# Inverting the triangular blocks of a gated DeltaNet with powers of one nilpotent factor in place of three doublings

## The chip, the cores and the metric

The kernel runs on one core of a Trainium2 chip. Its time is the device time of one execution in microseconds, and lower is better. A core has five engines, each with a queue of its own that runs in order: PE multiplies matrices, DVE, ACT and POOL work on vectors, and SP issues the transfers. A profile records one execution.

## What is computed

Two layers, each a mixer of three parts that run side by side on the same projection (S5, gated DeltaNet or GDN, Mamba-2), an output projection, and a feed-forward part: dense in layer 0, eight experts in layer 1. There are 256 latent tokens behind 256 context tokens, 1024 wide. The change lies in GDN. For each chunk it solves a triangular system:

```
lower = jnp.where(strict, jnp.einsum("bhnid,bhnjd->bhnij", kb, k) * decay, 0.0)
rhs = jnp.concatenate([v * beta[..., None], kb * jnp.exp(gc)[..., None]], axis=-1)
sol = lax.linalg.triangular_solve(jnp.eye(CHUNK, dtype=F32) + lower, rhs,
                                  left_side=True, lower=True, unit_diagonal=True)
```

The kernel uses chunks of 128 tokens, four of them (t = 0 to 3), in two directions (d = 0, 1), with four heads in one tile of 128 x 512. It inverts the 128 x 128 matrix I + L of each head, and then walks over the chunks with a state for each direction.

## The kernel before

A mixer (`mixer`) projects the inputs (lines 336 and 784: product, convolution, SiLU), prepares GDN (`gdn_prep`, which inverts the blocks of 16 on the diagonal), and then writes down, one after another, GDN, the decays of Mamba-2, the remaining projections, the modulation vectors, S5's readout, Mamba-2's outputs and the output projection. That is not the order in which they run. Each part has a number (`band`), and a scheduler builds from these numbers, from the buffers and from modelled times one fixed order for every engine. Names that occur below:

- `inverses` (line 919) inverts two pairs (t, d) at once, a group. GDN has four groups, `grs[0]` to `grs[3]`, and after them or between them `step`, which uses an inverse, and `outs`, which normalizes the outputs `gd_o` by `gd_rs` and writes them (`gd_y`) to `yD`. From the blocks of 16 (`iv_X`) three levels lead to 128: at each, X is transposed and scaled to `iv_Z` (ACT), multiplied with `gd_kw` and masked to `iv_Q` (DVE), multiplied with X and subtracted from it (DVE).
- `m2_decays` (line 1060) computes 16 tiles of decays `dq_W`, writes them to `WD` in DRAM, and takes two selects `dq_r` on POOL for each (line 776). Mamba-2's outputs read them as `m_W`.
- `ada` (line 181) loads 32 pieces of 512 KB of layer 0's modulation weights, with two buffers, and accumulates them on PE in one bank of PSUM.
- `s5_out` (line 629) reads S5's states (`s5U`, `s5X`, `s5V`) and writes its part of `yD` as `s5yy`.
- The output projection reads `yD` as `yr`, splits it to `yo`, and multiplies it with `wH` and `wL`.
- Beside the projections DVE does the convolution's multiply-adds (`cv_acc`, line 800), the split of loaded weights (`wL`, line 322) and S5's scan (`s5B`, lines 609 and 612).

Each part has its tiles in a pool, and a pool is placed in SBUF at a fixed address of each partition. The decays' pool is on one side and GDN's on the other:

```
with self.band(b0 + q_["gd"]):
    p, q = self.pool("gd", sb)
    self.gdn(l, p, kT, qT, vD, kD, prep, *sc, qss, sm, szD, yD, t0, b0)
    q.close()
    qt.close()
with self.band(b0 + q_["db"]):
    p, q = self.pool("dq", sa)
    self.m2_decays(p, sm, WD, first)
```

In layer 0 the pool `dq` lies at 84992 to 101376 and `gd` at 102464 to 146400 (bytes of a partition in the compiled program). In layer 1 they are apart as well.

Of the kernel before, what the change touches and what calls it, by code (L numbers as in the profile page):

```python
# [10 lines left out]
F32 = mybir.dt.float32  # L11
F32R = mybir.dt.float32r
I32 = mybir.dt.int32
AF = mybir.ActivationFunctionType
OP = mybir.AluOpType
# [12 lines left out]
U0, QKV0, ZG0, ZM0, XBC0 = 0, 512, 2048, 2576, 3600  # L28

CST = ["ident", "ones", "le", "ge", "gt", "lt", "blk16"]  # L30
LEVELS = [16, 32, 64]

Q0 = dict(
    pb=1.0, sc=2.5, tl=1.5, th=0.5, nb=7.5, db=1.9, ab1=0.85, ab2=3.0, sb=3.5, u=1.02, st=0.6, qkv=1.0, g0=2.0,
# [19 lines left out]
def _cst():  # L54
    i = np.arange(128)
    r, c = i[:, None], i[None, :]
    out = [r == c, np.ones((128, 128)), r <= c, r >= c, r > c, r < c, r // 16 == c // 16]
    for b in LEVELS:
        mf = ((r // b) % 2 == 1) & (c // b == r // b - 1)
        out += [mf, mf.T]  # L60
    c16 = np.arange(16)[None, :]
    out += [c16 == r % 16, c16 > r % 16, c16 < r % 16, (r // 16) % 2 == np.arange(2)[None, :]]
    return np.concatenate([np.asarray(m, np.float32) for m in out], axis=1)
# [27 lines left out]
class Net:  # L91
    def __init__(self, ctx, tc, A, out, dump=None):
        self.tc, self.nc, self.A, self.out, self.dump = tc, tc.nc, A, out, dump or {}
        nc = self.nc
        self.cpool = ctx.enter_context(tc.tile_pool(name="const", bufs=1))
        self.wstack = ctx.enter_context(ExitStack())
        self.wpool = self.wstack.enter_context(tc.tile_pool(name="wts", bufs=2, side="right"))
        self.dram = ctx.enter_context(tc.tile_pool(name="scr", bufs=1, space=DRAM))
        self.psum = ctx.enter_context(tc.tile_pool(name="psum", bufs=1, space=PSUM))
        self.psum_split(mm=(0, 1), px=(2, 3), bg=(4, 5, 6, 7), ad=(6, 7))  # L100
        c = self.cpool
        ncst = len(CST) + 2 * len(LEVELS)
        cst = c.tile([128, ncst * 128 + NC16], F32, name="cst")
        self.bands, self.ma, self.cur = {}, {}, None
        nm = len(CST) * 128
        nc.sync.dma_start(cst[:, 0:nm], A["cst"][:, 0:nm])
        with self.band(1.7):
            nc.sync.dma_start(cst[:, nm:], A["cst"][:, nm:])

        def mat(j):  # L110
            return cst[:, j * 128:(j + 1) * 128]

        for j, n in enumerate(CST):
            setattr(self, n, mat(j))
        self.mt = {}
        for j, b in enumerate(LEVELS):
            self.mt[b, 0] = mat(len(CST) + 2 * j)
            self.mt[b, 1] = mat(len(CST) + 2 * j + 1)
        c16 = cst[:, ncst * 128:]
        self.id16, self.up16, self.lo16, self.half16 = c16[:, 0:16], c16[:, 16:32], c16[:, 32:48], c16[:, 48:50]  # L120
        self.tri_r = c.tile([128, 2, 128], F32R, name="tri_r")
        nc.vector.tensor_copy(self.tri_r[:, 0, :], self.gt)
        nc.vector.tensor_copy(self.tri_r[:, 1, :], self.lt)
        self.pp = [c.tile([128, NPP], F32, name=f"pp{l}") for l in range(2)]
        for l in range(2):
            with self.band(0 if l == 0 else 1.7):
                nc.sync.dma_start(self.pp[l], A["pp"][l])
        self.epst = c.tile([128, 1], F32, name="epst")
        nc.vector.memset(self.epst, EPS)
        self.mods = [c.tile([128, 48, 2], F32, name=f"mods{l}") for l in range(2)]  # L130
        self.xT = c.tile([128, KT, T], F32, name="xT")
# [461 lines left out]
    def s5_scan(self, l, p, B, lam):  # L593
# [25 lines left out]
        for q in range(4):  # L619
            gs = slice(q * 8, q * 8 + 8)  # L620
            for x in range(2):
                X = p.tile([128, 8, 64], F32, name="s5X", tag="s5t", bufs=Q[l]["st_"])
                nc.scalar.activation(X[0:64], bv[0:64, x, gs], AF.Copy)
# [271 lines left out]
    def gdn(self, l, p, kT, qT, vD, kD, prep, nrm, bs, ks, qss, sm, szD, yD, t0, b0):  # L895


        nc = self.nc
        kw, qw, x16 = prep
        first = t0 // 128  # L900
        sh = [128, 4, 128]

        def v4(ps):
            return ps.rearrange("p (h c) -> p h c", h=4)

        def col(m):
            return m.unsqueeze(2).to_broadcast(sh)

        def mm4(lhs, rhs):
            ps = self.ps()  # L910
            for h in range(4):
                self.mm(ps[:, h * 128:(h + 1) * 128], lhs(h), rhs(h), start=True, stop=True, skip_group_check=True)
            return ps
# [4 lines left out]

        def inverses(gr):

            X = {}
            for t, d in gr:
                X[t, d] = p.tile(sh, F32, name="iv_X", bufs=Q[l]["iv"])
                nc.gpsimd.tensor_tensor(X[t, d].rearrange("p h (b c) -> p h b c", c=16),
                                        x16[d][:, 4 * t:4 * t + 4].unsqueeze(2).to_broadcast([128, 4, 8, 16]),
                                        self.blk16.rearrange("p (b c) -> p b c", c=16).unsqueeze(1).to_broadcast([128, 4, 8, 16]),
                                        op=OP.mult)
            for b in LEVELS:
                Z, W = {}, {}
                for t, d in gr:  # L930
                    pz = self.ps()
                    for h in range(4):
                        nc.tensor.transpose(pz[:, h * 128:(h + 1) * 128], X[t, d][:, h], self.ident)  # L933
                    Z[t, d] = p.tile(sh, F32, name="iv_Z", tag="iv_Z", bufs=2)
                    for h in range(4):
                        nc.scalar.activation(Z[t, d][:, h], pz[:, h * 128:(h + 1) * 128], AF.Copy, scale=bs[:, t, d, h:h + 1])
                for t, d in gr:
                    pq = mm4(lambda h: kw[t][:, h], lambda h: Z[t, d][:, h])
                    W[t, d] = p.tile(sh, F32, name="iv_Q", tag="iv_Q", bufs=2)
                    nc.vector.tensor_tensor(W[t, d], v4(pq), self.mt[b, d].unsqueeze(1).to_broadcast(sh), op=OP.mult)  # L940
                for t, d in gr:
                    px = mm4(lambda h: W[t, d][:, h], lambda h: X[t, d][:, h])
                    nc.vector.tensor_tensor(X[t, d], X[t, d], v4(px), op=OP.subtract)
            return X

        def load(t):
# [6 lines left out]
        def step(t, d, Y, last):  # L953
# [5 lines left out]
            if old is not None:  # L959
                pr = mm4(lambda h: kT[:, h, sl], lambda h: old[:, h])  # L960
                r = p.tile(sh, F32, name="gd_r", bufs=1)
# [3 lines left out]
            else:  # L965
                r = vp[t]
# [4 lines left out]
                    nc.scalar.activation(qs[:, h], pqs[:, h * 128:(h + 1) * 128], AF.Copy, scale=cs[:, h:h + 1])  # L971
            pw = mm4(lambda h: Y[:, h], lambda h: r[:, h])
            if not last:
                vk = p.tile(sh, F32, name="gd_vk", tag="iv_Q", bufs=2)
                nc.vector.tensor_tensor(vk, v4(pw), col(ks[:, t, d, :]), op=OP.mult)
                pu = mm4(lambda h: ktk[t][:, h], lambda h: vk[:, h])
                if old is not None:
                    nc.gpsimd.tensor_tensor(old, old, col(sm["tot"][:, d, t, 16:20]), op=OP.mult)
                    nc.vector.tensor_tensor(old, v4(pu), old, op=OP.add)
                else:  # L980
                    S[d] = p.tile(sh, F32, name=f"gd_S{d}", bufs=1)
                    nc.scalar.activation(S[d], v4(pu), AF.Copy)
# [24 lines left out]
        def outs(pair):  # L1007

            f = slice(pair[0], pair[1] + 1)
            for t in pair:  # L1010
                for h in range(4):
                    jk = p.tile([128, 128], F32, name="gd_jk", bufs=1)
                    nc.scalar.activation(jk, os[t][:, h], AF.Square, accum_out=oss[:, t, h:h + 1])
            nc.vector.tensor_scalar(ov[:, f], qss[:, f], EPS, 128.0 * 128.0 * EPS, op0=OP.add, op1=OP.mult)
            nc.vector.tensor_add(ov[:, f], ov[:, f], oss[:, f])
            self.rsqrt(p, rs[:, f], ov[:, f], [128, 2, 4], 1.0 / 128, 0.0)
            for t in pair:
                nc.gpsimd.tensor_tensor(os[t], os[t], rs[:, t, :].unsqueeze(2).to_broadcast(sh), op=OP.mult)
            c = slice(pair[0] * 128 - t0, (pair[1] + 1) * 128 - t0)
            for h in (0, 2):  # L1020
                po = self.ps()
                for i in range(2):
                    for j, t in enumerate(pair):
                        nc.tensor.transpose(po[:, (2 * i + j) * 128:(2 * i + j + 1) * 128], os[t][:, h + i], self.ident)
                y = p.tile([128, 2, 256], F32, name="gd_y", tag="iv_Z", bufs=2)
                nc.sync.dma_start(y, szD[:, h:h + 2, c])
                nc.vector.scalar_tensor_tensor(y, po.rearrange("p (h c) -> p h c", h=2), self.prm(l, "gng"), y, op0=OP.mult,
                                               op1=OP.mult)
                nc.sync.dma_start(yD[:, 4 + h:6 + h, c], y)
# [966 lines left out]
```

## Time and profile before

| | |
|---|---|
| median of three runs | 2483.29 us (2481.88 to 2485.01) |
| profiled execution | 2479.87 us, span 2478.1 us |
| mean granted clock of PE | 0.974 of full speed |
| busy, of the span | PE 93%, DVE 75%, ACT 57%, POOL 10% |
| layer 0's mixer | 0 to about 716 us, then the dense part |
| layer 1's mixer | about 1200 to 1640 us, then the experts |
| transfers | 543.86 MB, mean 219 GB/s |

An engine's busy share is a mean over stages that have different limits, so the rows below are taken stage by stage. A time such as 397.15 is counted from the span's start. A group of rows names a line of the kernel, the tile that is written, and behind the arrow the tiles that are read; a `bank` is a piece of PSUM.

### The profile page before, as it was taken

The page shows a single profiled execution, that of the slowest core. Times are in us where ns is not written, and L with a number is a line of the kernel's source. Part 1 is how long each engine was busy: PE and PEld are TensorE (multiplying, and loading weights), DVE is VectorE, ACT ScalarE, POOL GpSimd, SP SyncE. Part 2 cuts the span into 40 slices and gives each one's busy share as a digit, 9 for nine tenths or more (in the row PEclk, how much of TensorE's full clock was granted, in tenths as well). Part 3 has the DMA queues.
Part 4 walks back from the last instruction along what each step waited for, and adds up shares of the span by engine and source line. Part 5 has one row for each costly group of instructions (what it writes and reads, how often), then busy time and mean ns, then how long its engine had stood idle before and what let it go on. Part 6 is the DMA issues. An engine that isn't in the chain of part 4 may idle for free.

```text
span 2478.1 us, 36217 instructions
## 1 busy us (share of the span) xinstructions
PE 2296.1 (93%) x12886; PEld 1843.6 (74%) x12886; DVE 1868.1 (75%) x3138; ACT 1419.7 (57%) x2200; POOL 257.3 (10%) x332
## 2 busy tenths in 40 slices
PE   7999887898999999998998799889999999999998
PEld 4878675666767777886887677778887888888876
DVE  8887995576577773436679867678888888888887
ACT  4765475343335343235764844357777777677765
POOL 0011553212000000000021522100000000000000
PEclk9999998997999999998999899989999999999999
DMA  7443336994455755323444474478999999999994
GB/s 254 134 125 121 112 122 215 268 277 146 122 204 176 255 179 185 94 89 101 149 135 130 157 209 123 133 290 316 332 335 362 349 338 337 356 342 341 354 344 167
DMA packets 222378, 543.86 MB, mean 219 GB/s; under 512 B 25584, under 2 KB 105456, under 8 KB 186096
## 3 DMA queue, kind: packets, MB, share of 16 engines
q1 hardware_dynamic: 222192, 541.49, 63.7%
q8 instruction: 103, 1.69, 0.3%
q14 instruction: 83, 0.68, 0.1%
HBM read 487.87 MB, written 53.54 MB: 218 GB/s over the span
## 4 chain that ended last, share of the span: by engine, by line
PE 65%; DVE 6%; DMA 5%; ACT 4%; issue 3%; POOL 0%; SPq 0%; ACTq 0%; DVEq 0%; POOLq 0%
PE bank L162 62%; DMA ada<-in_ada_w_dram 1%; ACT mwH L1673 1%; DVE mwL L1674 1%; DVE wL L322 1%; PE bank L1761 1%; DMA wr<-in_w_in_dram 1%; DVE s5B L612 0%; DMA s5X<-XD 0%; DVE s5t L609 0%; DVE cv_acc L800 0%; DMA vD<-gd_tok 0%; PE bank L933 0%; DMA s5V<-VD 0%; DMA yr<-yD 0%
## 5 line engine op out<-in xcount | busy, mean ns | idle before, releaser
L1674 DVE TENSOR_TENSOR mwL<-mwr,mwH 128x2048 fp32r<-128x2048 f32 (+1 forms) x272 | 605.1, 2226 | 96.5 <-PE bank L162 60.3
L1673 ACT ACTIVATE mwH<-mwr 128x2048 fp32r<-128x2048 f32 (+1 forms) x272 | 508.2, 1869 | 201.6 <-PE bank L162 168.8
L321 ACT ACTIVATE wH<-wr 128x512 fp32r<-128x512 f32 (+2 forms) x388 | 232.8, 605 | 389.6 <-PE bank L162 241.2
L322 DVE TENSOR_TENSOR wL<-wr,wH 128x512 fp32r<-128x512 f32 (+2 forms) x388 | 267.0, 690 | 209.5 <-ACT wH L321 204.7
L162 PE MATMUL bank<-mwL,xeH 128*128 128x512 f32 (+1 forms) x768 | 292.7, 381 | 9.3 <-DVE mwL L1674 9.3
L162 PE MATMUL bank<-mwH,xeL 128*128 128x512 f32 (+1 forms) x768 | 288.1, 375 | 0.0
L162 PE MATMUL bank<-mwH,xeH 128*128 128x512 f32 (+1 forms) x768 | 284.7, 376 | 2.5 <-ACT mwH L1673 2.5
L162 PE MATMUL bank<-hH,wH 128*128 128x512 f32 (+2 forms) x656 | 245.8, 383 | 32.0 <-ACT cv_acc L798 18.6
L162 PE MATMUL bank<-hH,wL 128*128 128x512 f32 (+2 forms) x656 | 245.6, 376 | 8.7 <-DVE wL L322 8.5
L162 PE MATMUL bank<-hL,wH 128*128 128x512 f32 (+2 forms) x656 | 246.6, 376 | 1.1 <-DVE hL L300 1.1
L162 PEld LDWEIGHTS bank<-mwL,xeH 128*128 128x128 f32 x768 | 144.3, 188 | 37.7 <-DVE mwL L1674 11.7
L162 PEld LDWEIGHTS bank<-hH,wH 128*128 128x128 f32 (+1 forms) x656 | 124.0, 190 | 61.7 <-ACT cv_acc L798 20.7
L162 PEld LDWEIGHTS bank<-mwH,xeH 128*128 128x128 f32 x768 | 144.1, 188 | 32.3 <-ACT mwH L1673 3.3
L162 PEld LDWEIGHTS bank<-mwH,xeL 128*128 128x128 f32 x768 | 144.3, 188 | 26.3
L800 DVE SCALAR_TENSOR_TENSOR cv_acc<-cv_raw,pp,cv_acc 128x512 f32<-128x512 f32 (+1 forms) x192 | 152.8, 811 | 7.5 <-ACT cv_acc L796 5.8
L162 PEld LDWEIGHTS bank<-hH,wL 128*128 128x128 f32 (+1 forms) x656 | 124.4, 190 | 33.7 <-DVE wL L322 10.7
L162 PE MATMUL bank<-yo,wH 128*128 128x512 f32 (+1 forms) x512 | 133.2, 351 | 11.5 <-ACT yo L1387 7.7
L162 PEld LDWEIGHTS bank<-hL,wH 128*128 128x128 f32 (+1 forms) x656 | 124.7, 190 | 25.3 <-DVE hL L300 2.9
L162 PE MATMUL bank<-fhH,wH 128*128 128x512 f32 x352 | 137.6, 394 | 2.7 <-ACT fhH L299 1.8
L162 PE MATMUL bank<-mwL,eaH 128*128 128x512 f32 x352 | 139.2, 395 | 0.0
L162 PE MATMUL bank<-mwH,eaL 128*128 128x512 f32 x352 | 138.6, 394 | 0.0
L162 PE MATMUL bank<-fhL,wH 128*128 128x512 f32 x352 | 137.9, 392 | 0.0
(449 smaller groups left out, 4531.2 us busy)
## 6 DMA issues: line engine op xcount, KB each, us to landing
mwr<-in_moe_gu_dram SPq DMA_DIRECT2D x176, 1024.0 KB, 5.7
mwr<-in_moe_dn_dram SPq DMA_DIRECT2D x80, 1024.0 KB, 6.0
wr<-in_w_in_dram SPq DMA_DIRECT2D x160, 256.0 KB, 2.9
ada<-in_ada_w_dram SPq DMA_DIRECT2D x24, 1024.0 KB, 7.1
wr<-in_w_out_dram SPq DMA_DIRECT2D x64, 256.0 KB, 2.7
ada<-in_ada_w_dram SPq DMA_DIRECT2D x32, 512.0 KB, 6.0
wr<-in_ffn_w_gate_dram SPq DMA_DIRECT2D x44, 256.0 KB, 2.7
wr<-in_ffn_w_up_dram SPq DMA_DIRECT2D x44, 256.0 KB, 2.8
```

The costliest lines, as they stand in the source:

```text
L162: return self.nc.tensor.matmul(*a, **k)
L321: nc.scalar.activation(wH, w, AF.Copy)
L322: nc.vector.tensor_tensor(wL, w, wH.bitcast(F32), op=OP.subtract)
L800: nc.vector.scalar_tensor_tensor(acc, raw[:, :, j:j + 256], w[:, j:j + 1], acc, op0=OP.mult, op1=OP.add)
L1673: nc.scalar.activation(wH, w, AF.Copy)
L1674: nc.vector.tensor_tensor(wL, w, wH.bitcast(F32), op=OP.subtract)
L1761: nc.tensor.transpose(pt[:, j * 128:(j + 1) * 128], a[:, j * 128:(j + 1) * 128], self.ident)
```

## The change

The three levels become one. X, the inverse of the diagonal blocks, is transposed and scaled once. Two products of it with `gd_kw`, each masked by one of two new masks (all blocks of 16 above, or below, the diagonal), give a nilpotent matrix G (tag `iv_Q`) and its transpose F (tag `iv_Z`). G2 = G·G comes from one more product. Then X becomes X − GX, X + G2·X, and X + G2·(G2·X). The tags `iv_Z` and `iv_Q` have three buffers instead of two, and the constants hold two masks in place of six (128 x 306 instead of 128 x 818 floats).

```diff
-LEVELS = [16, 32, 64]
...
-    for b in LEVELS:
-        mf = ((r // b) % 2 == 1) & (c // b == r // b - 1)
-        out += [mf, mf.T]
+    out += [c // 16 > r // 16, c // 16 < r // 16]
...
-            for b in LEVELS:
-                Z, W = {}, {}
-                for t, d in gr:
-                    pz = self.ps()
-                    for h in range(4):
-                        nc.tensor.transpose(pz[:, h * 128:(h + 1) * 128], X[t, d][:, h], self.ident)
-                    Z[t, d] = p.tile(sh, F32, name="iv_Z", tag="iv_Z", bufs=2)
-                    for h in range(4):
-                        nc.scalar.activation(Z[t, d][:, h], pz[:, h * 128:(h + 1) * 128], AF.Copy, scale=bs[:, t, d, h:h + 1])
-                for t, d in gr:
-                    pq = mm4(lambda h: kw[t][:, h], lambda h: Z[t, d][:, h])
-                    W[t, d] = p.tile(sh, F32, name="iv_Q", tag="iv_Q", bufs=2)
-                    nc.vector.tensor_tensor(W[t, d], v4(pq), self.mt[b, d].unsqueeze(1).to_broadcast(sh), op=OP.mult)
-                for t, d in gr:
-                    px = mm4(lambda h: W[t, d][:, h], lambda h: X[t, d][:, h])
-                    nc.vector.tensor_tensor(X[t, d], X[t, d], v4(px), op=OP.subtract)
+            for t, d in gr:
+                pz = self.ps()
+                for h in range(4):
+                    nc.tensor.transpose(pz[:, h * 128:(h + 1) * 128], X[t, d][:, h], self.ident)
+                Z[t, d] = p.tile(sh, F32, name="iv_Z", tag="iv_Z", bufs=3)
+                for h in range(4):
+                    nc.scalar.activation(Z[t, d][:, h], pz[:, h * 128:(h + 1) * 128], AF.Copy, scale=bs[:, t, d, h:h + 1])
+            for t, d in gr:
+                pg = mm4(lambda h: kw[t][:, h], lambda h: Z[t, d][:, h])
+                G[t, d] = p.tile(sh, F32, name="iv_Q", tag="iv_Q", bufs=3)
+                nc.vector.tensor_tensor(G[t, d], v4(pg), self.off[1 - d].unsqueeze(1).to_broadcast(sh), op=OP.mult)
+                pf = mm4(lambda h: Z[t, d][:, h], lambda h: kw[t][:, h])
+                F[t, d] = p.tile(sh, F32, name="iv_F", tag="iv_Z", bufs=3)
+                nc.vector.tensor_tensor(F[t, d], v4(pf), self.off[d].unsqueeze(1).to_broadcast(sh), op=OP.mult)
+            for t, d in gr:
+                p2 = mm4(lambda h: F[t, d][:, h], lambda h: G[t, d][:, h])
+                G2[t, d] = p.tile(sh, F32, name="iv_G2", tag="iv_Q", bufs=3)
+                nc.scalar.activation(G2[t, d], v4(p2), AF.Copy)
+                px = mm4(lambda h: G[t, d][:, h], lambda h: X[t, d][:, h])
+                nc.vector.tensor_tensor(X[t, d], X[t, d], v4(px), op=OP.subtract)
+            for t, d in gr:
+                px = mm4(lambda h: G2[t, d][:, h], lambda h: X[t, d][:, h])
+                nc.vector.tensor_tensor(X[t, d], X[t, d], v4(px), op=OP.add)
+            for t, d in gr:
+                px = mm4(lambda h: G2[t, d][:, h], lambda h: X[t, d][:, h])
+                tt = p.tile(sh, F32, name="iv_T", tag="iv_Z", bufs=3)
+                nc.scalar.activation(tt, v4(px), AF.Copy)
+                Z[t, d] = tt
+            for t, d in gr:
+                px = mm4(lambda h: G2[t, d][:, h], lambda h: Z[t, d][:, h])
+                nc.vector.tensor_tensor(X[t, d], X[t, d], v4(px), op=OP.add)
```

The tags' other users, `gd_vk` and `gd_y`, get `bufs=3` too. No band and no other part is edited. In layer 0 the pool `dq` now lies at 82944 to 99328 and `gd` at 98368 to 146400. The second buffer of `dq_r` (95232 to 99328) thus shares 960 bytes with GDN's `gd_ncs`, `gd_oss`, `gd_ov`, `gd_rs` and the start of its first `iv_X`. In layer 1 they don't meet. The scheduler makes the order anew. Lines of the new kernel are six lower than before up to `inverses` (776 is 770), and ten higher behind it (1018 is 1028).

POOL before, in layer 0: the last 16 selects (`dq_r`) stand among the projections' `cv_raw` and ahead of the third group's blocks (`iv_X`); the other 16 stand further ahead.

```order
L791 MEMSET cv_raw 128x2x2
L776 AFFINE_SELECT dq_r<-la_793 128x1024 x2
L790 MEMSET cv_raw 128x2x2
L791 MEMSET cv_raw 128x2x2
L776 AFFINE_SELECT dq_r<-la_793 128x1024 x14
L924 TENSOR_TENSOR iv_X<-gd_x_2935,cst 128x512
L924 TENSOR_TENSOR iv_X<-gd_x_2930,cst 128x512
L988 AFFINE_SELECT gd_A<-gd_qw_2866 128x512 x2
L1127 TENSOR_TENSOR m_S_5965<-m_S_5957,ex 128x512
```

POOL with the change, in layer 0: `gd_A` and `gd_o` are GDN's last steps and outputs.

```order
L998 AFFINE_SELECT gd_A<-gd_qw_2924 128x512
L988 TENSOR_TENSOR gd_S_3538<-gd_S_3538,ex 128x512
L998 AFFINE_SELECT gd_A<-gd_qw_2924 128x512
L998 AFFINE_SELECT gd_A<-gd_qw_2895 128x512
L1011 TENSOR_TENSOR gd_o<-gd_o,gd_qs 128x512 x2
L1028 TENSOR_TENSOR gd_o<-gd_o,gd_rs 128x512 x2
L770 AFFINE_SELECT dq_r<-la_793 128x1024 x19
L1197 TENSOR_TENSOR m_z<-m_in,m_z 128x4x128
L770 AFFINE_SELECT dq_r<-la_793 128x1024 x7
L1197 TENSOR_TENSOR m_z<-m_in,m_z 128x4x128
L770 AFFINE_SELECT dq_r<-la_793 128x1024 x6
L1158 TENSOR_TENSOR m_yo<-m_yo 128x512 x2
```

All 32 selects now stand behind the last `gd_o` (line 1028, which reads `gd_rs`), with two of Mamba-2's `m_z` among them.

PE before, where GDN's third group begins in layer 0 (line 933 transposes X, `iv_Z,gd_kw` is the first product of a level, `iv_X,iv_Q` the second).

```order
L933 MATMUL bank_3607<-cst,iv_X 128x128 x4
L933 MATMUL bank_3617<-cst,iv_X 128x128 x4
L162 MATMUL bank_3627<-iv_Z,gd_kw_2884 128x128 x3
L162 MATMUL bank_5365<-ada,sc 32x256 x4
L162 MATMUL bank_3627<-iv_Z,gd_kw_2884 128x128
L162 MATMUL bank_3634<-iv_Z,gd_kw_2913 128x128 x4
L162 MATMUL bank_3641<-iv_X,iv_Q 128x128 x4
L162 MATMUL bank_5365<-ada,sc 32x256 x4
L162 MATMUL bank_5599<-s5D,s5U 64x128
L162 MATMUL bank_3647<-iv_X,iv_Q 128x128 x4
L933 MATMUL bank_3653<-cst,iv_X 128x128 x4
```

PE with the change, at the same place.

```order
L926 MATMUL bank_3555<-cst,iv_X 128x128 x4
L926 MATMUL bank_3565<-cst,iv_X 128x128 x4
L156 MATMUL bank_3575<-iv_Z,gd_kw_2884 128x128 x4
L156 MATMUL bank_3582<-gd_kw_2884,iv_Z 128x128 x4
L156 MATMUL bank_3596<-gd_kw_2913,iv_Z 128x128
L156 MATMUL bank_3603<-iv_Q,iv_F 128x128 x4
L156 MATMUL bank_3596<-gd_kw_2913,iv_Z 128x128 x2
L156 MATMUL bank_3589<-iv_Z,gd_kw_2913 128x128 x4
L156 MATMUL bank_3596<-gd_kw_2913,iv_Z 128x128
L156 MATMUL bank_3610<-iv_X,iv_Q 128x128 x4
L156 MATMUL bank_3616<-iv_Q,iv_F 128x128 x4
L156 MATMUL bank_3623<-iv_X,iv_Q 128x128 x4
```

The modulation (`ada`) and S5 (`s5D`, `s5V`) stood between the products before; now the group stands by itself, and those rows come behind GDN and the decays.

SP before, in layer 0: the last decay writes to `WD`, the modulation loads, and S5's `XD`.

```order
L190 DMA ada<-in_ada_w_dram 128x4x256 x2
L1067 DMA WD_3090<-dq_W 128x512 x2
L320 DMA wr<-in_w_out_dram 128x512
L1067 DMA WD_3090<-dq_W 128x512 x3
L1335 DMA mD_94<-cvo 128x512
L1067 DMA WD_3090<-dq_W 128x512
L190 DMA ada<-in_ada_w_dram 128x4x256 x2
L1067 DMA WD_3090<-dq_W 128x512
L190 DMA ada<-in_ada_w_dram 128x4x256
L626 DMA XD_1897<-s5X 128x512
L190 DMA ada<-in_ada_w_dram 128x4x256
```

SP with the change, at the last decay writes.

```order
L1077 DMA WD_3090<-dq_W 128x512 x2
L1105 DMA m_in<-mD_94 128x4x128
L1077 DMA WD_3090<-dq_W 128x512
L1107 DMA m_in<-mD_94 128x2x128
L1077 DMA WD_3090<-dq_W 128x512 x2
L184 DMA ada<-in_ada_w_dram 128x4x256 x2
L1209 DMA yD_90<-m_z 128x4x256
L1077 DMA WD_3090<-dq_W 128x512
L184 DMA ada<-in_ada_w_dram 128x4x256
L1168 DMA m_W<-WD_3090 128x512
L184 DMA ada<-in_ada_w_dram 128x4x256
```

Before, `ada` loads began ahead of the last seven writes, and GDN still had two groups to come. Now two `ada` loads stand far ahead, and the third stands behind 15 of the 16 writes; all of GDN's transfers stand ahead of these rows, and S5's `s5U` behind them. At the end of the stage, PE's 384 products of the output projection were mixed with Mamba-2's rows; they now stand behind the last of these and of `ada`.

## Rows read from the trace of the kernel before

**Rows 1.** The page, busy time, share of the span and instructions of each engine.
```profile
PE 2296.1 (93%) x12886; PEld 1843.6 (74%) x12886; DVE 1868.1 (75%) x3138; ACT 1419.7 (57%) x2200; POOL 257.3 (10%) x332
```

**Rows 2.** Windows: us; busy us (instructions) per engine; granted PE clock; DMA share, GB/s.
```profile
283.00:397.60 114.60, 87.47 (x434) 67.87 (x432) 114.60 (x150) 66.80 (x114) 66.44 (x57) 0.94 0.37 122
397.60:470.00 72.40, 62.99 (x528) 48.31 (x528) 31.76 (x55) 40.62 (x92) 13.21 (x13) 0.98 0.89 263
470.00:560.00 90.00, 82.49 (x654) 60.46 (x653) 59.43 (x132) 40.24 (x107) 16.81 (x15) 0.96 0.92 275
1440.00:1590.00 150.00, 134.49 (x1031) 112.20 (x1029) 100.28 (x211) 61.10 (x177) 31.36 (x29) 0.95 0.46 133
1700.00:2400.00 700.00, 689.79 (x3332) 569.26 (x3331) 607.03 (x390) 506.74 (x377) 0.00 (x0) 1.00 0.93 345
```

**Rows 3.** Windows, a piece with the transfer engines full.
```profile
500.00:515.00 15.00, 14.07 (x114) 9.35 (x113) 11.02 (x26) 4.96 (x17) 1.27 (x1) 1.00 1.04 306
```

**Rows 4.** Instructions of line 776: duration ns min/median/max, first and last start.
```profile
L776 POOL TENSOR_SCALAR_AFFINE_SELECT dq_r<-la x32: 1093/1540/3108, 282.6 to 392.8; 128x1024 fp32r<-128x1024 f32 x32
```

**Rows 5.** Groups of DVE, 301.5 to 397.7: busy us, mean ns, idle before.
```profile
L800 DVE SCALAR_TENSOR_TENSOR cv_acc<-cv_raw,pp,cv_acc 128x512 f32<-128x512 f32 x38 | 34.6, 922 | 0.0
L612 DVE TENSOR_TENSOR s5B<-s5B,s5t 128x512 f32<-128x512 f32 x18 | 16.1, 892 | 0.0
L322 DVE TENSOR_TENSOR wL<-wr,wH 128x512 fp32r<-128x512 f32 x17 | 16.0, 942 | 0.0
...
L940 DVE TENSOR_TENSOR iv_Q<-bank,cst 128x512 f32<-128x512 f32 x8 | 5.4, 678 | 0.0
```

**Rows 6.** Timeline of DVE, 359.5 to 364: start, duration.
```profile
359.95 0.74 DVE L800 SCALAR_TENSOR_TENSOR cv_acc<-cv_raw,pp,cv_acc 128x512 f32<-128x512 f32 x1
...
361.15 0.69 DVE L322 TENSOR_TENSOR wL<-wr,wH 128x512 fp32r<-128x512 f32 x1
```

**Rows 7.** Timeline of POOL, 385 to 397.
```profile
392.83 1.28 POOL L776 TENSOR_SCALAR_AFFINE_SELECT dq_r<-la 128x1024 fp32r<-128x1024 f32 x1 [0.15 <-PE bank L162]
```

**Rows 8.** Timeline of 396 to 410, one level of one group.
```profile
396.28 1.04 PE L933 MATMUL bank<-cst,iv_X 128*128 128x128 f32 x8
...
397.15 2.18 ACT L936 ACTIVATE iv_Z<-bank,gd_bs 128x128 f32<-128x128 f32 x8
...
401.55 2.05 PE L162 MATMUL bank<-iv_X,iv_Q 128*128 128x128 f32 x16
...
403.64 0.69 DVE L943 TENSOR_TENSOR iv_X<-iv_X,bank 128x512 f32<-128x512 f32 x1 [0.20 <-PE bank L162]
```

**Rows 9.** Groups of ACT, the table loads of one line.
```profile
L781 ACT ACT_TABLE_LOAD x23 | 29.5, 1283 | 5.6 <-issue 3.2 <-PE bank L162 2.1
```

**Rows 10.** Timeline of DVE, 1555 to 1585, layer 1's last steps.
```profile
1555.71 1.12 DVE L963 SCALAR_TENSOR_TENSOR gd_r<-bank,gd_ncs,gd_vp 128x128 f32<-128x128 f32 x4
...
1576.95 0.69 DVE L999 TENSOR_TENSOR gd_o<-bank,gd_o 128x512 f32<-128x512 f32 x1 [1.31 <-PE bank L162]
```

**Rows 11.** Timeline of POOL, 575 to 600.
```profile
582.57 2.18 POOL L1001 TENSOR_TENSOR gd_o<-gd_o,gd_qs 128x512 f32<-128x512 f32 x1 [4.32 <-DVE gd_o L999]
...
591.28 2.09 POOL L1018 TENSOR_TENSOR gd_o<-gd_o,gd_rs 128x512 f32<-128x512 f32 x2
```

**Rows 12.** Transfers of 397 to 570.
```profile
DMA packets 39368, 44.45 MB, mean 257 GB/s; under 512 B 2432, under 2 KB 31032, under 8 KB 39352
```

**Rows 13.** Instructions of line 641, 400 to 600.
```profile
L641 SPq DMA_DIRECT2D s5U<-UD x4: 319/376/682, 417.3 to 491.3; - x4
```

**Rows 14.** Instructions on the tile s5yy, 400 to 600.
```profile
L705 SPq DMA_DIRECT2D yD<-s5yy x4: 319/335/383, 547.2 to 559.8; - x4
```

**Rows 15.** Timeline of 598 to 609, all engines.
```profile
598.70 10.40 SPq L1386 DMA_DIRECT2D yr<-yD  x3
...
608.27 0.82 PE L162 MATMUL bank<-yo,wH 128*128 128x512 f32 x2
```

**Rows 16.** Windows, the instructions on the tile yo alone.
```profile
680.00:716.00 36.00, 35.95 (x151) 28.52 (x150) 0.70 (x1) 0.00 (x0) 0.98 0.28 85
```

More of the change, by code (lines that the diff above doesn't have):

```diff
@@ L101, in __init__ @@
         c = self.cpool
-        ncst = len(CST) + 2 * len(LEVELS)
+        ncst = len(CST) + 2
         cst = c.tile([128, ncst * 128 + NC16], F32, name="cst")
@@ L114, in __init__ @@
             setattr(self, n, mat(j))
[L115 to L118, printed above, removed]
+        self.off = [mat(len(CST)), mat(len(CST) + 1)]
         c16 = cst[:, ncst * 128:]
@@ L919, in inverses @@
         def inverses(gr):
-            X = {}
+            X, Z, F, G, G2 = {}, {}, {}, {}, {}
             for t, d in gr:
@@ L973, in step @@
             if not last:
-                vk = p.tile(sh, F32, name="gd_vk", tag="iv_Q", bufs=2)
+                vk = p.tile(sh, F32, name="gd_vk", tag="iv_Q", bufs=3)
                 nc.vector.tensor_tensor(vk, v4(pw), col(ks[:, t, d, :]), op=OP.mult)
@@ L1024, in outs @@
                         nc.tensor.transpose(po[:, (2 * i + j) * 128:(2 * i + j + 1) * 128], os[t][:, h + i], self.ident)
-                y = p.tile([128, 2, 256], F32, name="gd_y", tag="iv_Z", bufs=2)
+                y = p.tile([128, 2, 256], F32, name="gd_y", tag="iv_Z", bufs=3)
                 nc.sync.dma_start(y, szD[:, h:h + 2, c])
```

## The prediction

> **What bounds the kernel now.** I read the totals first: PE is busy 93% of the span, DVE 75% [rows 1]. So I cut the span at the stage borders [rows 2]. The reader is to see that no two stretches have the same limit. From 283 to 397.6 us, where layer 0's projections run beside GDN's first inverses, DVE is busy for all of 114.60 us and PE for 87.47: DVE sets the pace. From 397.6 to 560 PE does 145 of 162 us, with the DMA engines at 0.89 and 0.92: there GDN, the modulation (`ada`), S5's readout and Mamba-2's outputs share PE, and the loads of the latter three are the common work. A piece in which those engines are full moves 306 GB/s [rows 3]. In layer 1, 1440 to 1590 is PE work at 90%. The experts from 1700 are PE and transfers at once (689.79 of 700, 345 GB/s); no edit is there.
>
> Why is DVE full in the first stretch? All 32 selects of the decays (`dq_r`) run on POOL between 282.6 and 392.8 us, median 1540 ns [rows 4]. DVE operations that read both operands from SBUF take far longer beside them: L800 means 922 ns, L322 942 and L612 892 [rows 5]; where no select runs, L800 takes 0.74 and L322 0.69 [rows 6], and L612 of that width I put at 0.68. `iv_Q`, which reads one operand from PSUM, stays at 678 [rows 5]. The excess of these three is 38 x 0.18 + 17 x 0.25 + 18 x 0.21 = 15 us; with the narrower forms I put it at 20 (15 to 25). A select by itself takes 1.28 [rows 7].
>
> **The change, part by part.** Sixteen (t, d) pairs, eight a layer, are inverted.
> - PE. Per pair 12 transposes and 24 products become 4 and 28: in quads of four heads two quads of transposes less, one of products more. Two pairs' quads of products take 2.05 us, a pair's 1.03; two quads of transposes 1.04, one 0.52 [rows 8]. So 32 x 0.52 = 16.6 us go and 16 x 1.03 = 16.5 come: nothing.
> - DVE has 16 operations of 0.68 fewer, 11 us. On ACT 192 scaled copies (eight take 2.18 [rows 8]) become 64 and 32 plain ones of four heads each, no dearer in sum, and the order has 11 table loads of 1283 ns [rows 9] fewer, 14 us. ACT is busy for 58% of the first stretch and 41% of 1440 to 1590 [rows 2], so I count nothing for it; were its table loads all on the path, they'd give 14 us.
> - The chain. A level of one group runs from its transposes at 396.28 to the end of its second subtraction at 404.33 [rows 8], 8 us; three of them are 18 dependent stages and 24 us. The new form has 12 stages, so I estimate 16. Two groups of a layer stand behind the projections: 16 us a layer at most, nothing where other work fills the gaps.
> - The constants' first load shrinks by 0.26 MB: under 1 us at any rate shown.
>
> All of that is a gain of some us. The larger effect is one the diff doesn't name. The two tags with a third buffer take 4 KB more per partition, the constants 2 KB less, and in layer 0 the pool of the selects now overlaps GDN's by 960 bytes, at its `gd_rs` and first `iv_X`. `gd_rs` is read last by GDN's last operations. So the order puts all 32 selects behind the last `gd_o` on POOL, and on SP 30 of the 32 modulation loads behind 15 of the 16 writes of the decays; S5's readout and most of Mamba-2's outputs follow those. In layer 1 these pools don't overlap.
>
> Layer 0 then goes in sequence:
> 1. The DVE-bound stage starts at 283 and took 114.6 us. It loses the 20 of contention and gains some nine operations of 0.68 (6 us; group 1 and step 0 now end inside it): it ends near 384.
> 2. GDN with hardly a filler: two inverses at 16, and steps 1 to 3. In layer 1, where they stand close, the last two groups of steps take from 1555.71 to 1577.64 [rows 10], 22 us, 13 with states and 9 without. So 32 + 13 + 13 + 9 = 67. The outputs' tail, from `gd_o` L1001 to the end of L1018, takes 582.57 to 593.37, 10.8 [rows 11]. 384 + 78 = 462; I take 460 (450 to 470), as a group's steps and the next inverse overlap a little.
> 3. Thirty selects at 1.28 to 1.54 take 38 to 46 us, the dearer as Mamba-2's own DVE operations stand beside some, and the last write some us more: `ada` resumes near 502 (490 to 512).
> 4. The shared loads. The stretch 397 to 570 moves 44.45 MB [rows 12]; without `XD` (2.1), GDN's tiles (2.7) and the `m_W` that stand among the decay writes (1.3), and with two more `ada` (1.0), all by their sizes in the code, 39 remain. At 306 GB/s that is 128 us. S5's own chain, from its first `s5U` at 417.3 to the last `yD` write at 559.8, takes 142.5 [rows 13, 14], under the load of the rest. These two bound it; I take 134, as less stands beside the chain: the stage ends near 636.
> 5. From the first `yr` issue, 598.70, to the first product of the output projection, 608.27, pass 9.6 us [rows 15]. Its 384 products took 107 us with Mamba-2's rows between them; in the last stretch, with nothing between, 151 take 36 us [rows 16], so 384 take 91.5. It starts at 646 and ends at 737, where it ended at 715.6: +21 us. Nothing changes if it starts at 624.
>
> By the ends of steps 2 to 4 layer 0 is +10 to +35, and I take +21. Layer 1 keeps its order, and gains what of the chain's 16 us isn't filled: with PE at 90% in 1440 to 1590, 15 of those 150 us are idle at all, and I take half, -8 (0 to -15). Sum +13 on the profiled run of 2479.87, whose span is 2478.1; the median of the runs is 3.4 higher. Forecast: 2483.3 + 13 = 2496.
>
> The rows show what the selects cost DVE: 0.92 against 0.74, and 0.68 unmoved for the reader of PSUM [rows 5, 6]. The Trainium skill ("SBUF — State Buffer", Who interferes with whom) says that a DVE instruction with two SBUF inputs contends with a GpSimd instruction that reads SBUF, and one with at most one SBUF input doesn't. By that rule the selects would slow Mamba-2's two-operand products in their new place too, which is the 1.54 of step 3 rather than 1.28, some 8 us of the sum.
>
> **Rivals.**
> - *Faster.* The selects leave the DVE-bound stage, and what follows is quicker than I add it: `ada` resumes at 490 and the loads run at the experts' rate, 39 MB at 345 GB/s [rows 2], 113 us. Then the projection starts at 490 + 113 + 9.6 = 613, before 624: layer 0 gains 11, and layer 1 some 10. Time 2462. For it: the experts hold that rate for 700 us. Against it: with the engines full this stretch moved 306 [rows 3]. It decides from a projection start at 632 (624 and layer 1's 8).
> - *The same.* Layer 0 loses 4 to 12 and layer 1 wins it back: projection start 628 to 636, which `ada` at 490 and 306 GB/s give (490 + 128 + 9.6). Time 2483.
> - *Much slower.* S5's readout takes its chain and waits besides for the modulation loads on the one queue, so that the tail takes 160 us from 512. Start 682, layer 0 +58, layer 1 -4: 2537. For it: even with loads started early S5's chain took 142.5 [rows 13, 14]. Against it: the order keeps the three interleaved as before.
> - *No effect of the overlap.* The selects at their new place hide behind other work, as before. Then contention and chain alone are left, a time under the faster rival's. Against it is the order: behind the last `gd_o` little stands that does not itself wait for the selects. It shares the faster rival's chance.
>
> Where the experts' rate is argued, the Trainium skill ("DMA: Bandwidth & Descriptors", Bandwidth) gives 341 GB/s for 1 MB transfers and 138 for 64 KB, measured one at a time; by the first, an estimate, the 39 MB take 114 us. No run here shows single transfers.
>
> **How the numbers follow.** A measurement of this kernel tells 0.2%, 5 us, from nothing. Chances: forecast 0.56, faster rival 0.18, same 0.13, much slower 0.13. My forecast's own range is 2488 to 2516 (layer 0 +10 to +35, layer 1 near its middle). With 0.2 left out in all, part of the faster rival and part of the much slower one are cut: 2470 to 2524. Faster takes the faster rival and 0.02 of the forecast's low end, layer 1 at its best: 0.20. Same 0.13. Slower 0.67.
>
> **What the profile will show.** Right: `dq_r` on POOL in one run from near 460, L800 back to 0.74 in layer 0's projections, little `ada` and a low DMA share from 390 to 500, `ada` from near 500, the first output product between 630 and 660, then its products back to back; layer 1 shorter by some us. The forecast is wrong if `dq_r` starts well before 450, if the loads behind it reach 340 GB/s, or if GDN's chain without a filler has longer gaps than layer 1's steps let one think.

## The result

The changed kernel takes 2542.93 us (median of 4 runs, 2540.32 to 2544.43), the kernel before, run beside it, 2484.12: a ratio of 1.0242, with a 95% interval of 1.0229 to 1.0255. It is 59 us slower; the forecast was 13 slower, at most 40. The side was right, and so was the mechanism in layer 0; the size was not, and layer 1 went the other way. The profiled execution has a span of 2541.2 us, 63.1 more than before; 52.7 of these have come by the end of layer 0's output projection.

The page of the changed kernel, its row of busy times, beside [rows 1]:

```profile
PE 2327.1 (92%) x12886; PEld 1868.6 (74%) x12886; DVE 1841.2 (72%) x3122; ACT 1391.8 (55%) x2093; POOL 235.9 (9%) x332
```

DVE, ACT and POOL have 27, 28 and 21 us less to do; the sum had 31 for DVE, 14 for ACT's table loads and nothing for POOL. PE has as many records as before and is busy 31 us longer. The windows of the changed kernel, cut where its stages end (columns as in [rows 2]; the second and the third row are both GDN), show why:

```profile
283.00:378.00 95.00, 80.19 (x466) 68.91 (x466) 94.70 (x157) 36.52 (x71) 15.24 (x26) 0.96 0.32 106
378.00:400.00 22.00, 13.87 (x91) 12.84 (x90) 4.78 (x8) 20.79 (x33) 0.63 (x1) 0.88 0.23 84
400.00:483.00 83.00, 60.91 (x410) 53.64 (x410) 40.96 (x87) 27.52 (x90) 23.53 (x24) 0.83 0.27 86
483.00:536.00 53.00, 44.31 (x154) 26.48 (x158) 20.23 (x33) 17.00 (x31) 37.69 (x35) 0.69 0.39 130
536.00:669.00 133.00, 102.06 (x735) 63.21 (x724) 70.10 (x166) 45.18 (x93) 17.17 (x15) 0.82 0.94 283
677.00:768.00 91.00, 90.79 (x382) 72.22 (x382) 45.81 (x75) 30.66 (x45) 0.56 (x2) 0.98 0.39 122
```

The reader is to see five stages that stand one behind the other, where before GDN, modulation, S5 and the decays ran beside each other. In the rows from 400 and from 483 the DMA engines are at 0.27 and 0.39, and PE's mean granted clock is 0.83 and 0.69: PE has gaps, and part of the records behind them run at the lower of the clock's two levels, 1.2 instead of 2.4 GHz. Before, 397.6 to 560 had 0.96 to 0.98 [rows 2].

The selects of the changed kernel, by their line, answer to [rows 4], and DVE's groups from 301.5 to 378 to [rows 5]:

```profile
L770 POOL TENSOR_SCALAR_AFFINE_SELECT dq_r<-la x32: 1091/1092/1540, 483.2 to 534.8; 128x1024 fp32r<-128x1024 f32 x32
```

```profile
L794 DVE SCALAR_TENSOR_TENSOR cv_acc<-cv_raw,pp,cv_acc 128x512 f32<-128x512 f32 x36 | 26.1, 739 | 0.0
L606 DVE TENSOR_TENSOR s5B<-s5B,s5t 128x512 f32<-128x512 f32 x15 | 11.1, 744 | 0.0
L316 DVE TENSOR_TENSOR wL<-wr,wH 128x512 fp32r<-128x512 f32 x15 | 10.2, 679 | 0.3 <-ACT wH L315 0.3
```

All 32 have left the projections for the place behind GDN, and the convolution's operation fell from 922 to 739 ns, the split's from 942 to 679, S5's scan from 892 to 744.

### The profile page after: what moved, and what is told of

The parts are those of the page before. It is cut to its first block, busy times and chain, and to the rows that moved or that the text cites. A ratio compares the mean times of both kernels' runs of the same rounds, so it can differ in the third digit from the quotient of the medians.

```text
span 2541.2 us, 36130 instructions
## 1 busy us (share of the span) xinstructions
PE 2327.1 (92%) x12886; PEld 1868.6 (74%) x12886; DVE 1841.2 (72%) x3122; ACT 1391.8 (55%) x2093; POOL 235.9 (9%) x332
## 4 chain that ended last, share of the span: by engine, by line
PE 75%; DVE 8%; DMA 7%; ACT 6%; issue 2%; POOL 1%; SPq 1%; DVEq 0%; ACTq 0%; POOLq 0%
PE bank L156 72%; DMA ada<-in_ada_w_dram 2%; DVE wL L316 1%; DVE cv_acc L794 1%; ACT mwH L1683 1%; DVE mwL L1684 1%; DMA s5X<-XD 1%; DVE s5B L606 1%; PE bank L1771 1%; DMA s5V<-VD 1%; DVE s5t L603 1%; ACT s5X L617 1%; DMA yr<-yD 1%; ACT wH L315 1%; PE bank L506 1%
## 5 line engine op out<-in xcount | busy, mean ns | idle before, releaser
L156 PEld LDWEIGHTS bank<-mwL,xeH 128*128 128x128 f32 x768 | 144.4, 188 | 37.6 <-DVE mwL L1684 11.7
L794 DVE SCALAR_TENSOR_TENSOR cv_acc<-cv_raw,pp,cv_acc 128x512 f32<-128x512 f32 (+1 forms) x192 | 145.8, 775 | 13.1 <-ACT cv_acc L790 5.8
L156 PE MATMUL bank<-fhH,wL 128*128 128x512 f32 x352 | 138.2, 393 | 0.0
```

What stands on the lines that cost most here:

```text
L156: return self.nc.tensor.matmul(*a, **k)
L794: nc.vector.scalar_tensor_tensor(acc, raw[:, :, j:j + 256], w[:, j:j + 1], acc, op0=OP.mult, op1=OP.add)
```

## The experiments

Two theories. **O**: the 960 shared bytes put the decays behind GDN, and that order is the loss. **I**: the new inverses are themselves slower in their place. All ratios are to the kernel before, run on the same chip.

**Without the overlap, and what that edit costs alone.** `no_overlap` is the changed kernel and `dq_w_three` the kernel before, each with

```diff
-                W = p.tile([128, 4, 128], F32, name="dq_W", bufs=4)
+                W = p.tile([128, 4, 128], F32, name="dq_W", bufs=3)
```

> The changed kernel with three buffers for dq_W instead of four, so that the decays' pool ends 1 KB below GDN's pool in layer 0. Theory O (the 960 shared bytes put the decays behind GDN, and that order costs layer 0 its 52 us): the selects stand in the projections again, between 285 and 400 us, the output projection of layer 0 ends near 705 to 720, and the time is 2478 to 2500, the upper half if layer 1 keeps its own loss of 10 us. Rival I (the new inverses themselves are slower, since their chain waits for ACT and runs at a lower clock): layer 0 still ends near 750 or later and the time stays above 2520.

> The kernel before with three buffers for dq_W instead of four: what the edit of the run without overlap costs by itself. Both theories: no change, 2479 to 2489. If it is slower by more than 5 us, that much has to be taken off the run without overlap.

Measured: `no_overlap` 2498.42 against 2485.76 us, 1.0055 (1.0034 to 1.0076); `dq_w_three` 1.0004 (0.9991 to 1.0017). The selects of `no_overlap` are back in the projections, the last at 400. Of the 2.4% some 1.9 went with one buffer of 2 KB. But the output projection ended at 733, not by 720: there is a rest of 0.55%.

**The overlap with the old inverses, and its pair.** `overlap_old_inverses` is the kernel before with a third buffer for the tag `iv_Q` (of which `gd_vk` is the other user) in layer 0; `third_buffer_only` the same with three `dq_W`, so that the pools don't meet.

```diff
...
-tag="iv_Q", bufs=2
+tag="iv_Q", bufs=3 if l == 0 else 2
...
```

> The kernel before, with the three doublings, and only the tag iv_Q at three buffers in layer 0, which lets the two pools share the same 960 bytes. Theory O: all 32 selects run behind the last gd_o, from about 490 us on, layer 0's output projection ends 45 to 65 us later than before, and the time is 2528 to 2550. Rival I: a third buffer costs nothing, 2478 to 2490.

> The pair to the run with old inverses and the overlap: the same third iv_Q buffer in layer 0, and dq_W at three buffers, so that the pools don't meet. Theory O (the shared bytes alone cost the 73 us): 2480 to 2492, the selects in the projections. Rival: the third buffer itself rearranges GDN, and some of the 73 us stay: above 2500.

Measured: 2559.04 us, 1.0285 (1.0261 to 1.0310), 9 us above the range, and 2484.71, 0.9991 (0.9976 to 1.0006). The selects of the first, by their line, stand as in the changed kernel, those of the second as before:

```profile
L776 POOL TENSOR_SCALAR_AFFINE_SELECT dq_r<-la x32: 1092/1094/1547, 498.2 to 547.1; 128x1024 fp32r<-128x1024 f32 x32
```

```profile
L776 POOL TENSOR_SCALAR_AFFINE_SELECT dq_r<-la x32: 1087/1536/3108, 280.5 to 390.7; 128x1024 fp32r<-128x1024 f32 x32
```

So theory O holds, and I falls: the old inverses with the overlap are slower than the new ones with it, 1.0285 to 1.0242. Nor did the third buffer rearrange anything by itself: up to 716 us DVE, ACT and POOL of `third_buffer_only` have their records in the order of the kernel before, one for one.

What the new inverses gain where nothing fills GDN can't be read from this pair. The selects begin at 483.2 instead of 498.2, and that these 15 us are near the 16 that two shorter chains were to give is chance. With the old inverses ACT's copies of S5's states (L623 to L625) fall into the last level of the second group, whose two scaled copies stand 7.8 us apart:

```profile
380.49 1.14 ACT L936 ACTIVATE iv_Z<-bank,gd_bs 128x128 f32<-128x128 f32 x4
...
388.26 1.14 ACT L936 ACTIVATE iv_Z<-bank,gd_bs 128x128 f32<-128x128 f32 x4
```

So the third group begins there at 402.6 instead of 378.4, and from its beginning to the selects pass 95.6 us, less than the 104.8 of the changed kernel, where the same copies fall into the third group.

**Why GDN alone took 104 us and not 76.** Two suspects from the trace of the changed kernel. The first, PE's timeline: it stops for the outputs of chunks 0 and 1, with the fourth group's transposes (L926) queued behind them.

```profile
425.60 0.66 PE L926 MATMUL bank<-cst,iv_X 128*128 128x128 f32 x4
427.81 1.16 PE L156 MATMUL bank<-gd_kw,iv_Z 128*128 128x128 f32 x8 [1.56 <-ACT iv_Z L929]
434.47 0.69 PE L1034 MATMUL bank<-cst,gd_o 128*128 128x128 f32 x2 [5.50 <-POOL gd_o L1028]
...
437.21 1.12 PE L926 MATMUL bank<-cst,iv_X 128*128 128x128 f32 x4 [0.20 <-DVE gd_y L1037]
```

The second, ACT's timeline: in the third group's inverse its copies of G2 (`iv_G`, as the profile leaves numbers out) stand among the copies of S5's states.

```profile
391.49 0.63 ACT L618 ACTIVATE s5X<-s5B 64x256 f32<-64x256 f32 x1
392.02 0.61 ACT L619 ACTIVATE s5X<-s5B 64x256 f32<-64x256 f32 x1
392.66 0.60 ACT L940 ACTIVATE iv_G<-bank 128x512 f32<-128x512 f32 x1
393.28 1.09 ACT L617 ACTIVATE s5X<-s5B 64x512 f32<-64x512 f32 x1
...
399.49 0.61 ACT L619 ACTIVATE s5X<-s5B 64x256 f32<-64x256 f32 x1
400.12 0.60 ACT L940 ACTIVATE iv_G<-bank 128x512 f32<-128x512 f32 x1
```

The two copies `iv_G` of one group stand 7.5 us apart, with S5's copies between them. What the two cost is seen at the third and the fourth inverse, each taken from PE's first transposes to the end of DVE's last addition (L953):

```profile
378.36 1.70 PE L926 MATMUL bank<-cst,iv_X 128*128 128x128 f32 x8
...
410.69 0.68 DVE L953 TENSOR_TENSOR iv_X<-iv_X,bank 128x512 f32<-128x512 f32 x1
...
454.99 0.68 DVE L953 TENSOR_TENSOR iv_X<-iv_X,bank 128x512 f32<-128x512 f32 x1
```

The third takes 33.0 us and the fourth, from its transposes at 425.60, 30.1; the sum had 16 for each. `outs_behind` writes the outputs behind the fourth inverse, `s5_copies_pool` puts layer 0's three copies on POOL (the first is shown; layer 1's become ACT's `copy`, 1097 instead of 1112 ns), `outs_and_copies` does both; all keep the overlap.

```diff
-        if first == 0:
-            with self.band(b0 + Q[l]["gdo"]):
-                outs((0, 1))
         with self.band(b0 + Q[l]["gl3"]):
             Y.append(inverses(grs[3]))
+        if first == 0:
+            with self.band(b0 + Q[l]["gdo"]):
+                outs((0, 1))
```

```diff
-                nc.scalar.activation(X[0:64], bv[0:64, x, gs], AF.Copy)
...
+                (nc.gpsimd.tensor_copy if l == 0 else nc.scalar.copy)(X[0:64], bv[0:64, x, gs])
...
```

> The changed kernel with the outputs of chunks 0 and 1 written behind the fourth group's inverse in the program instead of ahead of it, nothing else. In the changed kernel PE stood still from 425.6 to 437 us for these outputs, with the fourth group's transposes queued behind them; the forecast's sum left them out. Theory S (the forecast's GDN term is short by that): GDN ends 8 to 12 us earlier, near 472, and everything behind it, so 2531 to 2537. Rival R (the outputs' latency is filled later in either place, or other waits take over): no change, 2539 to 2546.

> The changed kernel with layer 0's copies of S5's states (lines 617 to 619) on POOL instead of ACT. In the changed kernel ACT was busy for 20.8 of the 22 us from 378 to 400 with them, and the third group's inverse took 32 us instead of the 16 of the forecast. Theory A (ACT's queue holds up that inverse): it shrinks to 18 to 22 us, GDN ends near 472, and the time is 2529 to 2536. Rival R: the inverse is held up by PE's clock and its own waits, GDN ends at 480 or later: 2539 to 2546.

> The changed kernel, overlap kept, with both edits at once: outputs of chunks 0 and 1 behind the fourth inverse, and S5's copies on POOL. One alone brought GDN's end from 482 to 474, the other to 470. If these two are what the forecast's GDN term lacked, GDN ends at 458 to 464 (the forecast had 460) and the time is 2522 to 2534. If they cover the same wait, it ends at 468 to 472: 2534 to 2541.

Measured: 2540.14 (1.0230, 1.0200 to 1.0260), 2538.47 (1.0225, 1.0195 to 1.0255) and 2521.36 us (1.0138, 1.0103 to 1.0172). The last `gd_o` starts at 482.2 in the changed kernel and at 474.4, 470.0 and 465.4 in these. By the place of GDN's end the two add up to 17 of the 22 us by which the forecast of 460 was missed. So by GDN's end theories S and A hold. By the time they don't: the first lies in rival R's range, the second between the two. The times of the single edits don't tell them from the changed kernel beyond the intervals; that of both does, by 1%. That is more than 17 us, so the edits changed more than GDN's end; the granted clock from 381 to 466 is 0.94 with both, against 0.84 from 378 to 483 in the changed kernel. With the copies on POOL the third group runs without a stop, from its transposes at 378.3 to its last product's end at 394.1 and its last addition's at 394.9: the 16 us of the forecast, and 33.0 in the changed kernel. Rows of PE's and DVE's timelines in `s5_copies_pool`:

```profile
378.29 1.67 PE L926 MATMUL bank<-cst,iv_X 128*128 128x128 f32 x8
...
387.16 4.17 PE L156 MATMUL bank<-iv_X,iv_G 128*128 128x128 f32 x32
391.17 1.06 PE L156 MATMUL bank<-iv_T,iv_G 128*128 128x128 f32 x8
...
393.01 1.06 PE L156 MATMUL bank<-iv_T,iv_G 128*128 128x128 f32 x8
...
394.26 0.68 DVE L953 TENSOR_TENSOR iv_X<-iv_X,bank 128x512 f32<-128x512 f32 x1
```

With the outputs behind it the fourth group takes 17.8 us instead of 30.1. Rows of `outs_behind`:

```profile
427.30 0.60 PE L926 MATMUL bank<-cst,iv_X 128*128 128x128 f32 x4
...
444.37 0.69 DVE L953 TENSOR_TENSOR iv_X<-iv_X,bank 128x512 f32<-128x512 f32 x1
```

With both edits PE still stands for Mamba-2's loads (`m_in`) at the fourth group's beginning, and then does some 8 us of Mamba-2's rows until 432; no run takes these away.

```profile
413.24 1.11 PE L1112 MATMUL bank<-cst,m_in 128*128 128x128 f32 x4 [3.32 <-DMA m_in<-mD]
```

**The rest without the overlap.** PE's waits in `no_overlap`, 400 to 735:

```profile
PE bank L156 <- ACT yo L1397: 14.3, 2, 12.0
PE bank L156 <- DMA ada<-in_ada_w_dram: 8.0, 5, 3.0
```

PE waits once for 12.0 us for `yo`, which comes from Mamba-2's last outputs: the order has them late in the output projection. `no_overlap_m2_early` lowers Mamba-2's bands in layer 0, `m2_early_old` does that to the kernel before, and `all_mended` also writes the outputs behind the fourth inverse.

```diff
...
-m2=4.0, m2o=3.9, m2g=4.0
+m2=3.0, m2o=2.9, m2g=3.0
...
```

> The run without overlap, with Mamba-2's three bands one lower in layer 0 (m2 3.0, m2o 2.9, m2g 3.0), which puts its last outputs ahead of half the output projection as before, where without overlap PE waited 12 us for them. Theory M (the 14 us that the new inverses still cost without the overlap are this order, not the inverses): layer 0's output projection ends near 712 to 722, and the time is 2476 to 2488. Rival I (the inverses or their DVE work in the first stage cost it): it stays at 2492 to 2502.

> The control for the earlier Mamba-2 bands: the kernel before with m2 3.0, m2o 2.9, m2g 3.0 in layer 0. If the bands only mend the order that the new inverses upset, the kernel before gains nothing: 2480 to 2492. If they are an improvement by themselves, 2470 to 2479, and then the new inverses in layer 0 still cost some 10 us without the overlap.

> The new inverses in both layers, no overlap, Mamba-2's bands one lower in layer 0, and the outputs of chunks 0 and 1 behind the fourth inverse: the version that the runs so far point to. If the stall at these outputs counts without the overlap too, 2474 to 2484, under the kernel before. If modulation and S5 fill it there, as PE's waits without overlap say (1.4 us for gd_o), it is as the run with the earlier bands: 2482 to 2492.

Measured: 2487.14 (1.0009, 0.9992 to 1.0025), 2487.74 (1.0003, 0.9989 to 1.0017) and 2489.52 us (1.0015, 0.9998 to 1.0031). So 0.5% came from that order, which the scheduler made anew, and not from the inverses; what remains of both inverses and mended order is no gain either. In `m2_early_old` layer 0's output projection ended at 705 instead of 716, and the 10 us were given back behind it: no time can be read from one stage's end alone.

**Layer 1.** `new_in_layer1` has the new inverses there alone, with both sets of masks in the constants; `unused_masks` is its control, the old inverses with the same constants.

```diff
...
+        inverses = inverses_old if l == 0 else inverses_new
...
```

> The old inverses in layer 0 and the new ones in layer 1 alone (both sets of masks are loaded; no pools overlap). Theory O with a loss of layer 1 by its own order: layer 1 loses the 10 us that it lost in the changed kernel, 2489 to 2498. Rival L (layer 1's loss came with layer 0's, by what was late there, and the new inverses are cheaper): 2468 to 2484.

> The control for the run with the new inverses in layer 1 alone: the kernel before, old inverses in both layers, with the two unused masks loaded. That run was 12 us faster, and its profile has 10 of them in layer 0, whose code it left alone. If the shifted load and the order that it makes in layer 0 did that, this run gains 8 to 12: 2472 to 2478. If layer 1's inverses did it, it gains nothing: 2480 to 2489.

Measured: 2473.85 us, 0.9949 (0.9933 to 0.9966), and 2479.01, 0.9967 (0.9955 to 0.9979), between the two ranges. The first beats both kernels, but two thirds of its gain come with the two more masks alone, which nobody reads in the control. With these the order in layer 0 is another: up to 720 us, 190 of the 1254 records of DVE before stand elsewhere, and from the dense part to the experts none does. The difference, 5 us, is what layer 1's inverses may give; the intervals overlap a little.

## Why the prediction was wrong

- **The overlap and the order.** Right, and shown by the pair with the old inverses: selects behind GDN, `ada` from 536, then the sequence of the five steps. The steps' lengths, and layer 1, were not all right.
- **Step 1**, the DVE-bound stage to 384: it ended at 378, 19.6 us shorter than before instead of 14. With the 6 us of added operations as in the sum, the contention was worth some 25 us, the top of its range.
- **Step 2**, GDN to 460, is the step that failed: 482 from 378, 104 us instead of 76. Its term of two inverses at 16 was mis-sized: they took 33.0 and 30.1, 63 us for 32. The steps (34 for 35) and the last outputs' tail (8 for 11) were right. The fourth inverse waited for a tail of outputs that the sum had left out: it had one where layer 0 has two, although the listing has `outs((0, 1))` between the groups. The third waited for ACT: the sum took the chain from a level whose scaled copies found ACT free [rows 8], without a look at what the new order puts on ACT there, S5's 24 copies. The kernel before shows it one level on. The transposes are done at 406.25, and their scaled copies start at 411.96, behind S5's copies and a piece of the convolution:

```profile
405.16 1.09 PE L933 MATMUL bank<-cst,iv_X 128*128 128x128 f32 x8
405.60 1.08 ACT L623 ACTIVATE s5X<-s5B 64x512 f32<-64x512 f32 x1
...
411.96 2.18 ACT L936 ACTIVATE iv_Z<-bank,gd_bs 128x128 f32<-128x128 f32 x8
```

  Each edit brings its inverse back to 16 to 18 us, and GDN's end forward by 8 (`outs_behind`) and 12 (`s5_copies_pool`); both together gave 17. The rest I didn't separate; Mamba-2's rows and loads in the fourth group are in its place in the trace.
- **Step 3**, 38 to 46 us for the selects: 52 to 53, from 483.2 until `ada` at 536.3. Each select was cheaper than costed, 1.09, as the minimum of [rows 4] had said; the 1.28 of [rows 7] was not a select by itself. But the forecast took POOL's time for the period. The changed kernel's timeline shows two buffers in a ring:

```profile
488.32 2.14 POOL L770 TENSOR_SCALAR_AFFINE_SELECT dq_r<-la 128x1024 fp32r<-128x1024 f32 x2 [0.37 <-PE bank L156]
...
489.46 2.27 PE L156 MATMUL bank<-dq_r,tri_r 128*128 128x512 f32 x4 [0.24 <-POOL dq_r L770]
...
490.82 2.14 POOL L770 TENSOR_SCALAR_AFFINE_SELECT dq_r<-la 128x1024 fp32r<-128x1024 f32 x2 [0.36 <-PE bank L156]
...
492.04 1.47 DVE L1174 TENSOR_TENSOR m_E<-m_E,m_W 128x512 f32<-128x512 f32 x1 [6.40 <-DMA m_W<-WD]
...
513.84 0.74 PE L156 MATMUL bank<-dq_r,tri_r 128*128 128x512 f32 x2 [1.65 <-POOL dq_r L770]
...
516.04 0.68 DVE L1174 TENSOR_TENSOR m_E<-m_E,m_W 128x512 f32<-128x512 f32 x1
```

  A tile of decays takes 2.50 us: 2.14 for POOL's two selects, and 0.36 in which POOL waits for PE to release a buffer. PE needs 2.3 for four products at a granted clock of 0.50 (488 to 503); at 1.00 (510.4 to 515) two take 0.74. Sixteen tiles make 40; Mamba-2's rows between them on PE make up the rest, as POOL waits for PE 15.3 us in all. The contention with Mamba-2's operations, for which I took up to 1.54, is small: the median select has 1092 ns, and only single ones 1540. The Trainium skill ("SBUF — State Buffer", Who interferes with whom) says that a DVE instruction with two SBUF inputs contends with a GpSimd instruction that reads SBUF; the trace agrees where they meet, as `m_E` times `m_W` took 1.47 beside selects and 0.68 without, but they rarely meet there.
- **Steps 4 and 5** were right: `ada` at 536.3 to the last `s5yy` issue at 668.9 is 133 (forecast 134), at 283 GB/s; 7.7 us later the output projection starts, and its products take 91.7 (forecast 91.5). That the loads hit within 1 us is in part luck: they were 37.6 MB instead of 39, the rate was under the 306, S5's own chain took 124 instead of 142.5 (545.0 to 668.9), and 134 was a choice between the two bounds. So the projection ended at 768.3 instead of 737: 31 of the 50 us that the forecast was short in the profile, 22 by step 2's end and 12 by step 3, less 3 in steps 4 and 5. The other 18 are the dense part and layer 1.
- **Layer 1** was to gain 8 us and, with the dense part, lost 10.4. By the profiles, one of each run, that is not the inverses: measured from the dense part's first product to the experts' first, the five runs with the overlap, old inverses or new, have 943 to 950 us, the four with new inverses and no overlap 930 to 938, and the old ones without overlap 934 to 942 (951 with the earlier bands). Nor did layer 1 keep its order, as I had said: in `overlap_old_inverses`, whose layer 1 is that of the kernel before, 218 of the 1405 records of DVE in this stretch stand elsewhere than before. But the kernel before, `dq_w_three` and `unused_masks` have one order there, and take 934, 942 and 941: most of the 10 us is within what one order gives from one execution to the next. Their cause is open. In the changed kernel some 4 lie in the dense part and the rest in layer 1; which transfer or order carries them over I didn't try.
- **The rivals.** "Much slower" (2537) came nearest in time, but its mechanism, a tail of 160 us, did not occur: the tail was as forecast, and the delay stood ahead of it. The experts' rate was not reached: 283 GB/s.

## What to carry to other kernels

Where pools share SBUF, a few hundred bytes decide an order: compare the pools' addresses and the queues' order before and after any change of buffer counts, and leave a margin. When such a change strings stages together, cost each stage by its own critical ring, with what the new order puts on every engine in it, not by the busy time of one engine in a stage where others filled the gaps. And a gain of half a per cent in a scheduled kernel needs a control that changes the order alone.

## What was not expected of the hardware

A stage of dependent products with gaps loses twice: its waits, and PE's granted clock, which was 0.83 from 400 to 483 and 0.69 from 483 to 536 where the kernel before has 0.96 to 0.98 [rows 2]. In the changed kernel it fell while PE stood 7.9 us for GDN's last outputs, and in the decays it stayed down: from 488 to 503 PE was busy 13.26 of 15 us by its records, with a wait of 0.2 to 0.4 us in most tiles, at a granted clock of 0.50. It rose between 507 and 510.4 (mean 0.65), while PE ran from 505.15 to 510.05 without a wait. Two windows of the changed kernel (columns as in [rows 2]):

```profile
488.00:503.00 15.00, 13.26 (x31) 6.40 (x30) 1.47 (x1) 2.99 (x5) 11.71 (x11) 0.50 0.35 117
510.40:515.00 4.60, 2.51 (x10) 1.39 (x10) 3.52 (x6) 3.85 (x11) 4.60 (x5) 1.00 0.54 183
```

In the first, four products of the decays take 2.27 us; in the second, two take 0.74. So a PE that a profile shows as 88% busy can be at half its speed. Over the span PE was busy 31 us longer for as many records, at a mean of 0.956 instead of 0.974.
